# Two layers of a hybrid diffusion block: layer 1's modulation summed on VectorE during layer 0's FFN, and a token-major Fourier branch on half the spectrum

## The chip, the core and the metric

The kernel runs on one core of a Trainium2 chip. The metric is the device time of one execution in microseconds (us). Engines are named as in the profile: PE is TensorE's matrix multiply and PEld its weight load, DVE is VectorE, ACT is ScalarE, POOL is GpSimd, and SP is the sync engine, whose queue issues most DMAs.

## The reference, cut to what matters

Two layers work on 256 latent tokens and 256 context tokens of 1024 channels; in layer 1 the context feeds only keys and values. All is fp32.

```python
mod  = silu_c  @ w_mod + b_mod          # 6 blocks of 1024: sh1 sc1 gt1 sh2 sc2 gt2, for the latent tokens
modc = silu_cc @ w_mod[:, :n] + ...     # the same for the context: 6 blocks in layer 0, blocks 0 and 1 in layer 1
h    = modulate(x, g_norm1, sh1, sc1)   # rms_norm(x, g) * (1 + sc1) + sh1
proj = h @ w_in                         # keys/values, queries, Fourier columns (512), three gates
o_four = real(fft2(proj[fourier].reshape(b, l, 4, 128), axes=(tokens, channels of a group), norm="ortho"))
x = x + gt1 * (sum over MLA, GQA and Fourier of sigmoid(gate) * (o @ w_branch)) @ w_o
x = x + gt2 * conv_ffn(modulate(x, g_norm2, sh2, sc2))   # up (2 x 2816), width-3 conv, silu gate, down
```

The real part of a group's two-dimensional transform is C_tok F C_ch - S_tok F S_ch, with cosine and sine matrices over 256 tokens and 128 channels.

## The kernel before, in words

Tokens lie in the free dimension and channels on partitions for most of the work: 512 columns (latent and context) in layer 0, 256 in layer 1. Every large product is done in three matmuls, `mm3` (lines 104 to 106): each operand is split into a rounded part on ACT and a rest on DVE (`split`, lines 118 to 126), so each weight chunk of 128x1024 passes through one DMA of 512 KB, an ACT cast and a DVE subtraction. `wchunk` holds three raw chunks and three split ones. PSUM has eight banks under five tags: "mm", "s" and "pt" with two each, "o" and "tk" with one each.

**Modulation.** For a block of 1024 columns of w_mod the contraction over 1024 channels is eight slices k. `mod_burst` (line 238) takes two slices at a time, a quarter q of the block: two raw tiles of 128x1024, and for each slice four fp32 matmuls whose stationary operand is 32 columns of `cpad` (the two conditioning vectors, then others that are ignored) and whose outputs go to four groups of 32 partitions (line 254). Quarters are added into `row` on DVE (line 261), and after the fourth the row is transposed back to partitions, and b_mod is added (lines 269 to 274). Layer 0's blocks 0 and 1 are done at the very start by `mod_unit`. The others are handed to the layer as lists: "g" is emitted between the heads of the first attention (GQA), "m" between those of the second (MLA), "n1" and "n2" right after the first and second norm, and "f" behind every second column group of the FFN's up-projection. Layer 0 carries layer 1's block 1 in "n2" and its own block 5 and layer 1's block 0 in "f"; layer 1 carries its own blocks 2, 3, 4 and 5.

**Fourier branch.** In each of two halves (two groups of 128 channels) the columns are projected channel-major (`L0fp`), split, multiplied by the channel cosines and sines into `Y` (token-major, 128 tokens at a time), split, and then four products over tokens are summed for each 256 tokens into `Z`, which is split into the operand of the branch projection. The tables come through `load_dft` (line 1060): the channel table and four of 128x256 over tokens. Behind the branch in program order stand, in layer 0, the first attention with the Fourier gates `gF` ("mm" banks) and projections `bF` as fillers between heads; in layer 1, the latent projections ("mm" banks) and then the same.

**FFN.** In layer 0 the 22 column groups of the hidden width are done as 12, then their down-projection, then 10, then theirs; each down-projection runs over four chunks `mc` of 256 output channels. In the second one's last chunk the next layer's first norm starts between its two halves.

**Order.** A planner simulates the timeline and lays out each engine's instructions from it: on each engine the instruction that is ready and stands first in priority goes next, where priority is program order and `tc.high_priority(n)` lifts a part by n places. The order is fixed when the kernel is built; at run time every engine works through its list in order. Tiles with one tag share buffers in program order, so a new tile waits until the older one's readers are done.

Of the kernel before, what the change touches and what calls it, by code (L numbers as in the profile page):

```python
# [8 lines left out]
F32 = mybir.dt.float32  # L9
F32R = mybir.dt.float32r  # L10
# [20 lines left out]
RAWBUFS = 3  # L31
WBUFS = 3
RSQRT_MAGIC = 0x5F3759DF
MOD_AHEAD = 400


@with_exitstack
def hybrid_kernel(ctx: ExitStack, tc: tile.TileContext, a: dict, out: bass.AP):
# [196 lines left out]
    def mod_burst(l, blk, q, tags=None, bank="tk"):  # L235


        name = f"mod{l}"
        ps = pm(f"{name}_ps{blk}{q}", bank)
        raws = []  # L240
        for i in range(2):
            if tags:
                raw = S.tile([P, WMAX], F32, tag=tags[i], name=f"{name}_w{blk}{q}{i}")
            else:
                raw = wpool.tile([P, WMAX], F32, tag="mraw", name=f"{name}_w{blk}{q}{i}", bufs=2)
            k = 2 * q + i
            with after("qg0", l == 0 and blk == 2 and q == 0):
                nc.sync.dma_start(out=raw, in_=a["w_mod"][l, k * P:(k + 1) * P, blk * 1024:(blk + 1) * 1024])
            raws.append(raw)
        with tc.high_priority(MOD_AHEAD):  # L250
            for i in (1, 0):
                k = 2 * q + i
                for g in range(4):
                    nc.tensor.matmul(ps[32 * g:32 * g + 32, :256], cpad[:, 2 * k:2 * k + 32], raws[i][:, g * 256:(g + 1) * 256],  # L254
                                     start=i == 1, stop=i == 0, tile_position=(0, 32 * g))
        if q == 0:
            row = mod_rows[l, blk] = S.tile([P, 256], F32, tag="row", name=f"{name}_row{blk}", bufs=2)
            nc.scalar.copy(row, ps[:, :256])
# [148 lines left out]
    def layer(l, p, modT, last, xT, mods, prep, wkvg=None, norm=None):  # L407
# [146 lines left out]
        of_ = []  # L554
        with after("qg0"):
            dft = load_dft(l)
        for c in range(2):
            w = wchunk(w_in, 0, KD, FOUR_START + c * 256, 256, f"{n_}fo{c}")
            if last:
                ft = S.tile([P, 2, 2, TQ], F32R, tag=f"D{2 * c}", name=f"{n_}f{c}")  # L560
                fs = [ft[:, i] for i in range(2)]
            else:
                fs = [pair(f"D{2 * c + i}", f"{n_}f{c}{i}") for i in range(2)]
            fm_group(w, [0, P], KD, hs, TQ,
                     lambda i, ps: split(ps, fs[i][:, 0, :TQ], fs[i][:, 1, :TQ], later=True), f"{n_}fp{c}", "mm" if c == 0 else "o" if last else ("o", "tk"),
                     whole=lambda ps: split(ps.rearrange("p (i t) -> p i t", i=2), ft[:, :, 0, :], ft[:, :, 1, :]))
            Y = []
            for tt in range(NTQ):
                ps = pm(f"{n_}Y{c}{tt}", "s")
                ts = slice(tt * P, (tt + 1) * P)  # L570
                for i in range(2):
                    mm3(ps[:, i * 256:(i + 1) * 256], fs[i][:, 0, ts], fs[i][:, 1, ts],
                        dft[0][:, 0, :], dft[0][:, 1, :], True, True)
                y = pair(f"X{tt}", f"{n_}Y{c}{tt}")
                split(ps, y[:, 0, :], y[:, 1, :])
                Y.append(y)
            if last:
                zp = pm(f"{n_}Z{c}", "pt")
                zps = [zp[:, :TQ], zp[:, TQ:]]
            for i in range(2):  # L580
                ps = zps[i] if last else pm(f"{n_}Z{c}{i}", "pt")
                for s in range(NS):
                    n = 0
                    for t2 in range(2):
                        for cs in range(2):
                            y = Y[s * 2 + t2]
                            wsl = slice(i * 256 + cs * P, i * 256 + (cs + 1) * P)
                            q = 1 + t2 * 2 + cs
                            mm3(ps[:, s * 256:(s + 1) * 256], y[:, 0, wsl], y[:, 1, wsl],
                                dft[q][:, 0, :], dft[q][:, 1, :], n == 0, n == 3)  # L590
                            n += 1
                if not last:
                    o = pair(f"B{2 * c + i}", f"{n_}fo{c}{i}")
                    split(ps, o[:, 0, :], o[:, 1, :])
                    of_.append(o)
            if last:
                op = S.tile([P, 2, 2, TQ], F32R, tag=f"B{c}", name=f"{n_}fo{c}")
                split(zp.rearrange("p (i t) -> p i t", i=2), op[:, :, 0, :], op[:, :, 1, :])
                of_ += [op[:, 0], op[:, 1]]
# [341 lines left out]
        run_after(mods["n2"], before)  # L941
        nxt = []
        turn = None
        slots = ["B0", "B1", "B2", "B3", "D0", "D1", "D2", "D3", "D4", "Y0", "Y1", "E0", "E1"]
        per = 2 // NS
        for j0, jn in ((0, 12), (12, 10)) if not last else ((0, 22),):
            acts = []
            at_ = None
            for jj in range(jn):
# [42 lines left out]
                o = at_[:, jj % per]  # L992
                split(g[:, :TQ], o[:, 0, :], o[:, 1, :], 0.5)
                acts.append(o)
            for mc in range(4):
                ws = [wchunk(a["w_down"][l], j0 + k0, min(8, jn - k0), mc * 256, 256, f"{n_}dn{j0}{k0}{mc}")
                      for k0 in range(0, jn, 8)]

                def w(k, c, m):
                    return ws[k // 8](k % 8, c, m)  # L1000
                if last:
                    fm_group(w, [0, P], jn, acts, TQ, lambda i, ps: residual(mc * 2 + i, ps, 40),
                             f"{n_}dp{j0}{mc}", ("mm", "s")[mc % 2])
                    store(xn, mc)
                elif mc == 3 and j0:
                    fm_halves(w, [0, P], jn, acts, lambda i, s_, ps: residual_half(mc * 2 + i, s_, ps, 40), f"{n_}dp{j0}{mc}",
                              lambda: nxt.append(next_norm(xn)))
                else:
                    fm_group(w, [0, P], jn, acts, TQ, lambda i, ps: residual(mc * 2 + i, ps, 40),
                             f"{n_}dp{j0}{mc}", ("mm", "s")[mc % 2])  # L1010
# [48 lines left out]
    def load_dft(l):  # L1059

        d4 = S.tile([P, 2, 2, 256], F32R, tag="D4", name=f"dft{l}d")
        ts = [d4[:, 0], d4[:, 1]] + [S.tile([P, 2, 256], F32R, tag="pr", name=f"dft{l}{i}", bufs=3) for i in range(3)]
        for i, t in enumerate(ts):
            if i == 0:
                src = a["dft_d"]
            else:
                t2, cs = divmod(i - 1, 2)
                src = a["dft_s"][t2 * P:(t2 + 1) * P, cs * 256:(cs + 1) * 256]
            raw = S.tile([P, 256], F32, tag="ot", name=f"dft{l}r{i}", bufs=2)
            nc.sync.dma_start(out=raw, in_=src)  # L1070
# [22 lines left out]
    def next_norm(xn):  # L1093
# [3 lines left out]

    xT, nxt = layer(0, prm[0], modT[0], False, xT, {
        "n1": [], "g": bursts(0, 2) + bursts(0, 3), "m": bursts(0, 4),
        "n2": bursts(1, 1, (0, 1), ["Y0", "Y1", "Y2", "Y3"], "pt") + bursts(1, 1, (2, 3), None, "pt"),  # L1100
        "f": bursts(0, 5) + bursts(1, 0)}, [prep], w3)
    layer_params2(1, prm[1])
    layer(1, prm[1], modT[1], True, xT, {
        "n1": bursts(1, 2, (0, 1), ["Y1", "Y2", "Y3", "E1"], "pt"), "g": bursts(1, 2, (2, 3)) + bursts(1, 3), "m": bursts(1, 4),
        "n2": bursts(1, 5, range(4), free[8:], "pt"), "f": []}, [], None, nxt[0])

def _tables():
# [13 lines left out]
    def dft(n):  # L1123
# [38 lines left out]
```

## Time and profile before

| | us |
|---|---|
| median of 3 runs | 1423.36 (1422.74 to 1425.29) |
| profiled execution | 1422.24 |
| its span | 1420.4 |
| PE busy | 1379.5 |
| DVE busy | 892.4 |
| ACT busy | 662.2 |
| POOL busy | 332.9 |

The span runs from the first to the last instruction of the profiled execution. Busy times of different engines overlap. A matmul's recorded duration includes its way through the pipeline, so the distance between the starts of neighbours is the pace at which they are done, and the recorded duration is not.

### The profile page before, as it was taken

Reading aid. Unit: us, or ns where it says so; the run is one execution under the profiler, and the core shown is the slowest. Engines: PE = TensorE matmul, PEld = TensorE weight load, DVE = VectorE, ACT = ScalarE, POOL = GpSimd, SP = SyncE. Lnnn points to the kernel's source line nnn. Section 1 sums busy time; section 2 is a strip of 40 time slices with the busy share of each in tenths; the row PEclk is TensorE's granted clock in tenths of the full one; section 3 lists DMA queues with packets and bytes.
Section 4 is the critical chain, followed back from the end, with each engine's and each line's share of the span. In section 5 each row is a group of like instructions: output and inputs, shape, how many; then the busy total and the mean of one; then the engine's idle time right before and its main releaser. Section 6 shows DMA issues by size and latency. Waiting matters only on the chain.

```text
span 1420.4 us, 23006 instructions
## 1 busy us (share of the span) xinstructions
PE 1379.5 (97%) x8801; PEld 1195.3 (84%) x8801; DVE 892.4 (63%) x1644; ACT 662.2 (47%) x1164; POOL 332.9 (23%) x399
## 2 busy tenths in 40 slices
PE   6999999999999999999999999999998998999998
PEld 4988888878888788878678888899977998899998
DVE  5575655666645666655326663677687766788853
ACT  4434545435554344444114442445564663566642
POOL 3211323364323311101000111121245332112200
PEclk9999999999999999999999999999999999999999
DMA  9733442143321745343343232363744555466663
GB/s 318 247 89 105 148 146 73 54 120 106 90 74 38 262 149 197 101 148 104 104 134 91 87 99 91 111 177 95 229 134 140 155 176 188 129 180 186 184 191 121
DMA packets 163064, 197.97 MB, mean 139 GB/s; under 512 B 7144, under 2 KB 149530, under 8 KB 162954
## 3 DMA queue, kind: packets, MB, share of 16 engines
q1 hardware_dynamic: 161952, 195.85, 44.5%
q0 software_dynamic: 864, 0.61, 0.4%
q8 instruction: 69, 1.13, 0.3%
q14 instruction: 41, 0.34, 0.1%
q10 hardware_dynamic: 138, 0.04, 0.0%
HBM read 192.28 MB, written 3.15 MB: 138 GB/s over the span
## 4 chain that ended last, share of the span: by engine, by line
PE 89%; DVE 5%; DMA 2%; POOL 1%; issue 1%; ACT 1%; SPq 1%; DVEq 0%; ACTq 0%; POOLq 0%
PE L0upp L104 6%; PE L0upp L105 6%; PE L0upp L106 6%; PE mod_ps L254 3%; PE L1upp L104 3%; PE L1upp L105 3%; PE L1upp L106 3%; PE L0dp L106 3%; PE L0dp L104 3%; PE L0dp L105 3%; PE L0gp L106 3%; PE L0gp L104 3%; PE L0gp L105 3%; PE L1dp L106 1%; PE L1dp L104 1%; PE L1dp L105 1%
## 5 line engine op out<-in xcount | busy, mean ns | idle before, releaser
L104 PE MATMUL L0upp<-L0n_h,L0up_h 128*128 128x512 f32 (+1 forms) x384 | 141.7, 373 | 1.1 <-ACT L0n_h L332 1.1
L105 PE MATMUL L0upp<-L0n_h,L0up_h 128*128 128x512 f32 (+1 forms) x384 | 141.9, 373 | 0.0
L106 PE MATMUL L0upp<-L0n_h,L0up_l 128*128 128x512 f32 (+1 forms) x384 | 140.0, 373 | 0.0
L984 POOL TENSOR_TENSOR L0sg<-L0sg,L0u 128x512 f32<-128x512 f32 x22 | 31.4, 1426 | 288.6 <-DVE L0u L961 274.9
L104 PE MATMUL L1upp<-L1n_h,L1up_h 128*128 128x256 f32 x352 | 96.5, 286 | 1.1 <-ACT L1n_h L332 1.1
L106 PE MATMUL L1upp<-L1n_h,L1up_l 128*128 128x256 f32 x352 | 97.0, 285 | 0.0
L105 PE MATMUL L1upp<-L1n_h,L1up_h 128*128 128x256 f32 x352 | 96.4, 285 | 0.0
L124 DVE TENSOR_TENSOR L0up_l<-L0up_w,L0up_h 128x1024 fp32r<-128x1024 f32 x44 | 58.8, 1337 | 53.7 <-ACT L0up_h L118 50.6
L104 PEld LDWEIGHTS L0upp<-L0n_h,L0up_h 128*128 128x128 f32 x384 | 71.8, 188 | 15.4 <-issue 1.6
L106 PEld LDWEIGHTS L0upp<-L0n_h,L0up_l 128*128 128x128 f32 x384 | 72.1, 188 | 13.6 <-issue 0.8
L105 PEld LDWEIGHTS L0upp<-L0n_h,L0up_h 128*128 128x128 f32 x384 | 72.0, 188 | 13.5 <-issue 0.8
L118 ACT CAST L0up_h<-L0up_w 128x1024 fp32r<-128x1024 f32 x44 | 46.3, 1053 | 72.2 <-PE L0upp L105 49.7
L104 PE MATMUL L0gp<-L0n_h,L0g_h 128*128 128x512 f32 x192 | 76.3, 397 | 0.0
L105 PE MATMUL L0gp<-L0n_h,L0g_h 128*128 128x512 f32 x192 | 75.5, 393 | 0.0
L106 PE MATMUL L0gp<-L0n_h,L0g_l 128*128 128x512 f32 x192 | 75.2, 396 | 0.1
L106 PE MATMUL L0dp<-L0act,L0dn_l 128*128 128x512 f32 (+1 forms) x196 | 72.7, 371 | 0.0
L104 PE MATMUL L0dp<-L0act,L0dn_h 128*128 128x512 f32 (+1 forms) x196 | 72.6, 370 | 0.0
L105 PE MATMUL L0dp<-L0act,L0dn_h 128*128 128x512 f32 (+1 forms) x196 | 72.5, 370 | 0.0
L104 PEld LDWEIGHTS L1upp<-L1n_h,L1up_h 128*128 128x128 f32 x352 | 66.9, 194 | 1.5 <-ACT L1n_h L332 1.5
L106 PEld LDWEIGHTS L1upp<-L1n_h,L1up_l 128*128 128x128 f32 x352 | 67.3, 194 | 0.0
L105 PEld LDWEIGHTS L1upp<-L1n_h,L1up_h 128*128 128x128 f32 x352 | 66.8, 194 | 0.0
L124 DVE TENSOR_TENSOR L1up_l<-L1up_w,L1up_h 128x1024 fp32r<-128x1024 f32 x44 | 54.2, 1231 | 18.6 <-ACT L1up_h L118 17.2
(1534 smaller groups left out, 4322.9 us busy)
## 6 DMA issues: line engine op xcount, KB each, us to landing
mod_w<-in_w_mod_dram SPq DMA_DIRECT2D x96, 512.0 KB, 5.0
L0up_w<-in_w_up_dram SPq DMA_DIRECT2D x44, 512.0 KB, 3.6
L1up_w<-in_w_up_dram SPq DMA_DIRECT2D x44, 512.0 KB, 4.3
L0g_w<-in_w_in_dram SPq DMA_DIRECT2D x24, 512.0 KB, 3.7
L1g_w<-in_w_in_dram SPq DMA_DIRECT2D x24, 512.0 KB, 4.0
L0dn_w<-in_w_down_dram SPq DMA_DIRECT2D x20, 512.0 KB, 3.5
L1dn_w<-in_w_down_dram SPq DMA_DIRECT2D x16, 512.0 KB, 3.5
L0wo_w<-in_w_o_dram SPq DMA_DIRECT2D x8, 512.0 KB, 7.0
```

Source lines behind the costliest of these rows:

```text
L104: nc.tensor.matmul(ps, lh, rh, start=start, stop=False)
L105: nc.tensor.matmul(ps, lh, rl, start=False, stop=False)
L106: last_mm[0] = nc.tensor.matmul(ps, ll, rh, start=False, stop=stop).ins
L118: nc.scalar.copy(hi, src)
L124: nc.vector.tensor_sub(lo, src, f(hi))
L254: nc.tensor.matmul(ps[32 * g:32 * g + 32, :256], cpad[:, 2 * k:2 * k + 32], raws[i][:, g * 256:(g + 1) * 256], start=i == 1, stop=i == 0, ...
L984: nc.gpsimd.tensor_mul(g[:, :TQ], g[:, :TQ], us[1][:, :TQ])
```

## The change

Of layer 1's six modulation blocks, 0 to 4 are no longer bursts. For each slice k of 128 channels, DVE multiplies the raw 128x1024 weights by that slice's conditioning value, one per partition, and adds this to an accumulator; after eight slices the array sums the accumulator over its partitions with a column of ones (`opad`, shifted by one column per vector). Blocks 1 and 0 do it for two vectors, blocks 2, 3 and 4 for one, since layer 1 uses them for the latent tokens only. The 40 steps are emitted in layer 0's FFN: one behind each odd column group, and up to four ahead of each down-projection chunk. Layer 0's block 5 moves to its second norm; layer 1 keeps two quarters of its block 5 after each norm. `MOD_AHEAD` goes from 400 to 3000.

In the Fourier branch the projection is token-major, 512 columns at once. The token transform comes first, on a table of 129 cosine and 127 sine columns, into A (channels on partitions, half the spectrum's cosines and sines over tokens). The channel transform follows, as a product with the channel sines (`zs`) and one with the channel cosines (`zc`). Their sum gives tokens 1 to 127, their difference the mirrored tokens 255 to 129, and tokens 0 and 128 are copied.

```diff
-MOD_AHEAD = 400
+MOD_AHEAD = 3000
...
+    def mod_sums(l, blk, nv):
+        name = f"mod{l}"
+        accs = []
+        def step(k):
+            raw = wpool.tile([P, WMAX], F32, tag="mraw", name=f"{name}_w{blk}{k}", bufs=2)
+            nc.sync.dma_start(out=raw, in_=a["w_mod"][l, k * P:(k + 1) * P, blk * 1024:(blk + 1) * 1024])
+            if k == 0:
+                accs[:] = [S.tile([P, 1024], F32, tag=f"Y{2 + v}", name=f"{name}_acc{blk}{v}") for v in range(nv)]
+            for v, acc in enumerate(accs):
+                cv = cpad[:, 2 * k + v:2 * k + v + 1]
+                if k == 0:
+                    nc.vector.tensor_scalar(acc, raw, cv, None, ALU.mult)
+                else:
+                    nc.vector.scalar_tensor_tensor(acc, raw, cv, acc, op0=ALU.mult, op1=ALU.add)
+            if k < KD - 1:
+                return
+            ps = pm(f"{name}_ps{blk}", "tk")
+            with tc.high_priority(MOD_AHEAD):
+                for v, acc in enumerate(accs):
+                    for g in range(4):
+                        nc.tensor.matmul(ps[32 * g:32 * g + 32, :256], opad[:, 1 - v:33 - v], acc[:, g * 256:(g + 1) * 256],
+                                         start=v == 0, stop=v == nv - 1, tile_position=(0, 32 * g))
+            row = S.tile([P, 256], F32, tag="row", name=f"{name}_row{blk}", bufs=2)
+            nc.scalar.copy(row, ps[:, :256])
...
+        return [lambda k=k: step(k) for k in range(KD)]
...
-        for c in range(2):
...
+        w = wchunk(w_in, 0, KD, FOUR_START, 512, f"{n_}fo")
+        pss = [pm(f"{n_}fp{tt}", ("mm", "s")[tt // 2]) for tt in range(NTQ)]
+        for k0 in range(0, KD, 2):
+            for tt in range(NTQ):
+                ts = slice(tt * P, (tt + 1) * P)
+                for k in (k0, k0 + 1):
+                    wh, wl = w(k, 0, 512)
+                    mm3(pss[tt], hs[k][:, 0, ts], hs[k][:, 1, ts], wh, wl, k == 0, k == KD - 1)
+        ft = [pair(f"D{tt}", f"{n_}f{tt}") for tt in range(NTQ)]
+        for tt in range(NTQ):
+            split(pss[tt], ft[tt][:, 0, :], ft[tt][:, 1, :])
+        nb = 2 * NS
+        pss = [pm(f"{n_}A{b}", ("pt", "pt", "o", "tk")[b] if not last else "s") for b in range(nb)]
+        for s in range(NS):
+            for g in range(4):
+                b, hf = (g, s) if NS == 2 else divmod(g, 2)
+                gs = slice(g * P, (g + 1) * P)
+                for t2 in range(2):
+                    f_ = ft[s * 2 + t2]
+                    mm3(pss[b][:, hf * 256:(hf + 1) * 256], f_[:, 0, gs], f_[:, 1, gs],
+                        dft[1 + t2][:, 0, :], dft[1 + t2][:, 1, :], t2 == 0, t2 == 1)
+        As = [pair(f"X{b}", f"{n_}A{b}") for b in range(nb)]
+        for b in range(nb):
+            split(pss[b], As[b][:, 0, :], As[b][:, 1, :])
+        for b in range(nb):
+            ah, al = (As[b][:, i, :].rearrange("p (s k) -> p s k", s=2) for i in range(2))
+            zc = pm(f"{n_}Zc{b}", "mm" if not last else "pt")[:, :260].rearrange("p (s k) -> p s k", s=2)
+            zs = pm(f"{n_}Zs{b}", "s" if not last else ("o", "tk")[b])[:, :256].rearrange("p (s k) -> p s k", s=2)
+            mm3(zs, dft[0][:, 0, P:], dft[0][:, 1, P:], ah[:, :, P:], al[:, :, P:], True, True)
+            mm3(zc, dft[0][:, 0, :P], dft[0][:, 1, :P], ah[:, :, :130], al[:, :, :130], True, True)
+            zt = S.tile([P, 256], F32, tag="ot", name=f"{n_}zt{b}", bufs=2).rearrange("p (s k) -> p s k", s=2)
+            nc.scalar.copy(zt, zs)
+            z = S.tile([P, 512], F32, tag="pr", name=f"{n_}z{b}", bufs=3)
+            z3 = z.rearrange("p (s k) -> p s k", s=2)
+            nc.vector.tensor_add(z3[:, :, 1:P], zc[:, :, 1:P], zt[:, :, 1:])
+            nc.vector.tensor_sub(z3[:, :, 255:P:-1], zc[:, :, 1:P], zt[:, :, 1:])
+            nc.scalar.copy(z3[:, :, 0:P + 1:P], zc[:, :, 0:P + 1:P])
...
+                if j % 2:
+                    sums(1)
             for mc in range(4):
                 ws = [wchunk(a["w_down"][l], j0 + k0, min(8, jn - k0), mc * 256, 256, f"{n_}dn{j0}{k0}{mc}")
                       for k0 in range(0, jn, 8)]
+                sums(4)
...
-        "n2": bursts(1, 1, (0, 1), ["Y0", "Y1", "Y2", "Y3"], "pt") + bursts(1, 1, (2, 3), None, "pt"),
-        "f": bursts(0, 5) + bursts(1, 0)}, [prep], w3)
+        "n2": bursts(0, 5, (0, 1), ["Y0", "Y1", "Y2", "Y3"], "pt") + bursts(0, 5, (2, 3), None, "pt"), "f": [],
+        "v": [s for blk, nv in ((1, 2), (0, 2), (2, 1), (3, 1), (4, 1)) for s in mod_sums(1, blk, nv)]}, [prep], w3)
...
-        "n1": bursts(1, 2, (0, 1), ["Y1", "Y2", "Y3", "E1"], "pt"), "g": bursts(1, 2, (2, 3)) + bursts(1, 3), "m": bursts(1, 4),
-        "n2": bursts(1, 5, range(4), free[8:], "pt"), "f": []}, [], None, nxt[0])
+        "n1": bursts(1, 5, (0, 1), ["Y1", "Y2", "Y3", "E1"], "pt"), "g": [], "m": [],
+        "n2": bursts(1, 5, (2, 3), free[8:12], "pt"), "f": [], "v": []}, [], None, nxt[0])
```

## Rows read from the trace of the kernel before

**Rows 1.** The page: span, busy time by engine, chain of waits by engine.

```profile
span 1420.4 us, 23006 instructions
...
PE 1379.5 (97%) x8801; PEld 1195.3 (84%) x8801; DVE 892.4 (63%) x1644; ACT 662.2 (47%) x1164; POOL 332.9 (23%) x399
...
PE 89%; DVE 5%; DMA 2%; POOL 1%; issue 1%; ACT 1%; SPq 1%; DVEq 0%; ACTq 0%; POOLq 0%
```

**Rows 2.** Timeline of PE, layer 0's Fourier branch: start us, us, instruction.

```profile
107.80 0.39 PE L106 MATMUL L0gp<-L0n_h,L0g_l 128*128 128x512 f32 x1
...
108.71 0.39 PE L104 MATMUL L0gp<-L0n_h,L0g_h 128*128 128x512 f32 x1
108.94 0.28 PE L104 MATMUL L0Z<-dft0d,L0Y 128*128 128x256 f32 x1
...
110.85 0.28 PE L104 MATMUL L0Z<-dft,L0Y 128*128 128x256 f32 x1
```

**Rows 3.** Busy us (instructions) by stretch; then clock, DMA share, GB/s.

```profile
80.00:118.00 38.00, 38.00 (x241) 34.48 (x240) 24.30 (x40) 15.99 (x26) 4.97 (x10) 1.00 0.24 70
560.00:860.00 300.00, 300.00 (x1337) 237.91 (x1336) 158.15 (x194) 108.50 (x133) 27.80 (x20) 1.00 0.36 111
640.00:740.00 100.00, 100.00 (x422) 74.61 (x421) 38.92 (x50) 24.85 (x28) 5.75 (x4) 1.00 0.36 112
980.00:1046.00 66.00, 65.80 (x544) 58.57 (x544) 46.71 (x88) 40.02 (x82) 16.33 (x16) 1.00 0.59 186
1066.00:1092.00 26.00, 20.29 (x157) 18.06 (x156) 19.74 (x33) 10.20 (x17) 14.77 (x15) 0.95 0.55 171
1092.00:1172.00 80.00, 79.78 (x647) 74.69 (x646) 56.51 (x100) 49.72 (x96) 27.40 (x26) 0.99 0.49 151
```

**Rows 4.** Timeline of PE, one burst and the matmul behind it.

```profile
122.83 1.07 PE L254 MATMUL mod_ps<-mod_w,cpad 128*32 128x256 f32 x16
123.83 0.50 PE L104 MATMUL L0bp<-L0fo,L0b_h 128*128 128x512 f32 x1
```

**Rows 5.** The bursts alone (line 254) by stretch; 16 records are one burst.

```profile
980.00:1140.00 160.00, 10.71 (x160) 4.17 (x160) 0.99 0.53 161
```

**Rows 6.** Timeline, layer 1's second norm.

```profile
1213.88 1.96 PE L254 MATMUL mod_ps<-mod_w,cpad 128*32 128x256 f32 x32
...
1214.65 0.87 DVE L914 SCALAR_TENSOR_TENSOR L1xk<-L1o,modT,L1xk 128x256 f32<-128x256 f32 x2
...
1215.76 0.38 PE L316 MATMUL L1n_ss<-ones,L1n_sa 128*128 128x1 f32 x2
...
1220.45 0.70 PE L326 MATMUL L1n_rb<-L1n_dg,ones 128*128 128x256 f32 x2 [0.40 <-DVE L1n_dg L325]
```

**Rows 7.** Groups on DVE, 560 to 900 us: busy us, mean ns, idle before.

```profile
L124 DVE TENSOR_TENSOR L0up_l<-L0up_w,L0up_h 128x1024 fp32r<-128x1024 f32 x37 | 49.5, 1337 | 47.2 <-ACT L0up_h L118 46.9
...
L983 DVE SCALAR_TENSOR_TENSOR L0sg<-L0sg,L0u 128x512 f32<-128x512 f32 x19 | 13.1, 688 | 8.3 <-ACT L0sg L982 8.3
...
L261 DVE TENSOR_TENSOR mod_row<-mod_row,mod_ps 128x256 f32<-128x256 f32 x4 | 1.7, 414 | 5.5 <-PE mod_ps L254 5.5
```

**Rows 8.** Groups on DVE, 440 to 480 us.

```profile
L124 DVE TENSOR_TENSOR L0wo_l<-L0wo_w,L0wo_h 128x1024 fp32r<-128x1024 f32 x4 | 7.2, 1818 | 0.0
```

**Rows 9.** The token transform's result tile in layer 0: ns min/median/max.

```profile
L104 PE MATMUL L0Z<-dft,L0Y x24: 280/283/283, 97.5 to 116.1; 128*128 128x256 f32 x24
...
L104 PE MATMUL L0Z<-dft0d,L0Y x8: 277/283/283, 94.8 to 113.5; 128*128 128x256 f32 x8
...
L124 DVE TENSOR_TENSOR L0fo<-L0Z,L0fo x4: 690/691/691, 102.6 to 117.3; 128x512 fp32r<-128x512 f32 x4
```

**Rows 10.** Chain of waits, layer 1's first norm: start us, us, what.

```profile
920.07 0.24 PE L1kvg L105
...
926.07 0.13 PE L1kvg L104
```

**Rows 11.** What PE waited for: us in total, times, longest.

```profile
PE L1m0tq L872 <- POOL L1qtok L460: 4.6, 2, 2.5
```

More of the change, by code (lines that the diff above doesn't have):

```diff
@@ L275, in mod_burst @@
         return turn
+    def mod_sums(l, blk, nv):
[22 more added lines that the diff above has]
+            nc.scalar.copy(row, ps[:, :256])
+            tp = ps[:, 256:]
+            n = 96 + nv
+            for j in range(2):
+                nc.tensor.transpose(tp[:, j * P:j * P + n], row[:n, j * P:(j + 1) * P], ident[:n, :n])
+            for v in range(nv):
+                nc.vector.tensor_add(
+                    modT[l][:, v, blk * 8:(blk + 1) * 8].rearrange("p (g j) -> p j g", j=2),
+                    tp.rearrange("p (j g r) -> p j g r", j=2, g=4)[:, :, :, v],
+                    prm[l]["vec"][:, blk * 8:(blk + 1) * 8].rearrange("p (g j) -> p j g", j=2))
+        return [lambda k=k: step(k) for k in range(KD)]
     def scale_shift(l, sc0, sh0, g, nv):
@@ L556, in layer @@
             dft = load_dft(l)
-        for c in range(2):
-            w = wchunk(w_in, 0, KD, FOUR_START + c * 256, 256, f"{n_}fo{c}")
+        w = wchunk(w_in, 0, KD, FOUR_START, 512, f"{n_}fo")
[6 more added lines that the diff above has]
+                    mm3(pss[tt], hs[k][:, 0, ts], hs[k][:, 1, ts], wh, wl, k == 0, k == KD - 1)
@@ L559, in layer @@
             if last:
-                ft = S.tile([P, 2, 2, TQ], F32R, tag=f"D{2 * c}", name=f"{n_}f{c}")
-                fs = [ft[:, i] for i in range(2)]
-            else:
[L563 to L599, printed above, removed]
+                op = S.tile([P, 2, 2, TQ], F32R, tag=f"B{b}", name=f"{n_}fo{b}")
+                split(z3, op[:, :, 0, :], op[:, :, 1, :])
+                of_ += [op[:, 0], op[:, 1]]
+            else:
+                o = pair(f"B{b}", f"{n_}fo{b}")
+                split(z, o[:, 0, :], o[:, 1, :])
+                of_.append(o)
@@ L943, in layer, with sums @@
         turn = None
+        def sums(n):
+            for step in mods["v"][:n]:
+                step()
+            del mods["v"][:n]
         slots = ["B0", "B1", "B2", "B3", "D0", "D1", "D2", "D3", "D4", "Y0", "Y1", "E0", "E1"]
@@ L1034, in hybrid_kernel @@
     nc.vector.tensor_mul(cpk, csrc, cth)
+    opad = const.tile([P, 33], F32, name="opad")
+    nc.vector.memset(opad, 0.0)
+    nc.vector.memset(opad[:, 1:2], 1.0)
     xt0 = [S.tile([P, 2, 512], F32, tag=f"X{i}", name=f"x0{i}") for i in range(4)]
@@ L1061, in load_dft @@
         d4 = S.tile([P, 2, 2, 256], F32R, tag="D4", name=f"dft{l}d")
-        ts = [d4[:, 0], d4[:, 1]] + [S.tile([P, 2, 256], F32R, tag="pr", name=f"dft{l}{i}", bufs=3) for i in range(3)]
+        ts = [d4[:, 0], d4[:, 1], S.tile([P, 2, 256], F32R, tag="pr", name=f"dft{l}", bufs=3)]
         for i, t in enumerate(ts):
@@ L1066, in load_dft @@
             else:
-                t2, cs = divmod(i - 1, 2)
-                src = a["dft_s"][t2 * P:(t2 + 1) * P, cs * 256:(cs + 1) * 256]
+                src = a["dft_s"][(i - 1) * P:i * P, :]
             raw = S.tile([P, 256], F32, tag="ot", name=f"dft{l}r{i}", bufs=2)
@@ L1132, in _tables @@
         "dft_d": np.concatenate([cd, sd], axis=1).astype(np.float32),
-        "dft_s": np.concatenate([cs, -ss], axis=1).astype(np.float32),
+        "dft_s": np.concatenate([cs[:, :129], -ss[:, 1:128]], axis=1).astype(np.float32),
     }
```

## The prediction

> **What bounds the kernel now.** I read the page's busy shares first, then the chain of waits, then the stretches, then single instructions. The page shows TensorE (PE) busy 97% of the 1420.4 us, VectorE (DVE) 63%, and a chain that ended last of which 89% is PE [rows 1]. A PE that is busy need not be at its peak, so the paces come from the timeline: 128x512 matmuls start every 0.227 us (107.80 to 108.71 are four of them) and 128x256 ones every 0.12 us (108.94 to 110.85 are sixteen) [rows 2]. In layer 0's FFN and in most of layer 1's attention PE has no gap: 300.00 of 300, 65.80 of 66, 79.78 of 80 us; only 1066 to 1092 has a hole of 5.7 us [rows 3]. So this kernel's time is the sum of its matmul paces plus some 41 us (1420.4 - 1379.5) in which PE waits, and an edit is worth what it takes out of PE in a stretch without gaps.
>
> **The profiled execution.** It took 1422.24 us around a span of 1420.4; the median of the runs shown is 1423.36, 1.1 us more. I sum against 1422.2 and add 1.1 at the end.
>
> **Modulation: what goes.** Today a quarter of a 1024-column block is a "burst": 8 fp32 matmuls, recorded as 16, that take 1.00 us of PE (122.83 until the next matmul at 123.83) [rows 4]. Of layer 1's 24 bursts the change keeps block 5's four. Blocks 0 to 4, 20 bursts, become sums on DVE. Each block ends in four fp32 matmuls per conditioning vector: blocks 1 and 0 (two vectors) 8, as many as one burst, 1.0 us; blocks 2, 3, 4 (one vector) 4, 0.5 us if the pace holds; it can't be under that share, and a whole burst's 1.0 bounds it above. I take 2 x 1.0 + 3 x 0.5 = 3.5 us (up to 5.0): the same four column tiles in the same order. The transposes at a block's end stay as many, only earlier.
>
> In layer 0's FFN 12 bursts stand now: layer 1's block 1 beside the norm, layer 0's block 5 and layer 1's block 0 further on. Afterwards four remain (block 5, in block 1's old place). So -8 + 3.5 = **-4.5 us**, PE having no gap there [rows 3].
>
> In layer 1's attention 10 go, the 160 records at 980 to 1140 [rows 5]: six are handed to the first attention, four to the second. I take nine to lie where PE is full and one in or beside the stretch in which PE waits anyway. So **-9 us** (between 0, if VectorE and GpSimd set that stretch, and -10).
>
> At layer 1's second norm four bursts become two. They are fill: the last projection's residual on DVE starts at 1214.65 while two bursts run, the sums of squares start only at 1215.76, the other two bursts run while DVE works out the square root, and PE still waits 0.40 us before the broadcast at 1220.45 [rows 6]. I cost the removal at **0** (at best -0.8: two of DVE's 0.41 us row additions [rows 7] leave the chain). DMA: the same 512 KB loads, 24 more of them on the sync engine's queue in the FFN, 12 fewer in layer 1's attention and norm; with buffers two deep, and weights three deep in front of PE, I count none.
>
> **Modulation: what comes.** 40 steps, 16 with two DVE instructions and 24 with one: 56 of 128x1024 fp32. The trace has no such sum. The nearest in form is the 128x512 scalar_tensor_tensor in SBUF, 0.688 us; the nearest in width is the 128x1024 split, 1.34 us in the FFN [rows 7], 1.82 us at 440 to 480 where GpSimd is busy [rows 8]. I take 1.34: 75 us; bounds 56 x 0.688 = 39 and 56 x 1.82 = 102. In the FFN's stretch from 560 to 860 DVE is busy 158.1 of 300 us [rows 3], so 142 us stand idle there, plus the tail; 75 fits, 102 fits. The tightest place is the first down-projection, where 20 steps are issued, 10 of them double: 30 x 1.34 = 40 us on top of 38.9 in 100 [rows 3] (the stretch reaches a little past it). PE takes a weight chunk every 24 x 0.227 = 5.4 us and three chunks are held, so a sum in front of a split delays it inside its slack. The price on the path is **0**; if the cover goes, each sum that a needed split waits behind costs its 1.34 us.
>
> **Fourier branch, layer 0.** The projection becomes token-major: 96 matmuls of 512 columns before and after. Behind it, before: 48 (channel transform) + 96 (token transform) of 256 columns; the second group's rows stand three times each, 3 x 24 + 3 x 8 [rows 9]. After: 48 + 24 (12 of 256, 12 of 260). 72 fewer x 0.12 = -8.6 us. DVE and ACT keep about the same: 16 evacuations of 512 columns go to 12, and three half-width additions or copies plus a narrow one come for each of four groups; two table loads and their splits go.
>
> What is lost: slack. Now the gates of the Fourier branch fill PE between the transform's matmuls (0.227 us steps up to 108.71, the transform from 108.94) [rows 2], since they take the "mm" banks, which the transform does not use. Afterwards the cosine half sits in those two banks, so group 2 waits until group 0 is combined, and the gates wait until groups 2 and 3 are. One group costs DVE 0.69 (split in) [rows 9] + 2 x 0.42 (the 128x256 addition of the bursts, 0.415 [rows 7]) + 0.69 (split out) = 2.2 us against PE's 6 x 0.12 = 0.72. Four groups: 8.9 us of DVE from the end of the first, 2.1 us of PE in the rest of the first transform and 2.9 in the second. Splits out may be late, which leaves 6.1 us of DVE against 5.0 of PE, and the copies on ScalarE run ahead of it. So 1.1 us at least, 3.9 at most without filler; a burst (1 us), transposes and other heads fill some. I take a stall of 2.5: **-6.1 us**. Bounds: no stall, -8.6; a stall of 6 with weight splits between, -2.6.
>
> **Fourier branch, layer 1.** Half the tokens: 72 become 36, -36 x 0.12 = -4.3; the projection's 96 of 256 become 48 of 512, 96 x 0.12 - 48 x 0.227 = -0.6. Its second half uses other banks than the latent projections that follow, so I charge 1.5 us of latency: **-3.4 us** (0 to -4.9).
>
> **Sum.** -4.5 - 9 - 0 - 6.1 - 3.4 = -23.0. 1422.2 - 23.0 = 1399.2, plus 1.1: **1400 us**.
>
> **Rivals.**
> *A, everything is filled.* The planner lays bursts and other heads into the Fourier gaps and the norm gains its 0.8: -4.5 - 10 - 0.8 - 8.6 - 4.9 = -28.8, 1394.5. For it: PE shows no gap at all in today's branch (38.00 of 38) [rows 3]. Against: the shared banks.
>
> *B, the Fourier gaps grow until the clock falls.* Stalls of 6 and 4 us in place of 2.5 and 1.5, and after each a stretch at the lower clock. In layer 1's first norm PE waited 1.83 and 1.18 us, and its 288-column matmuls then came every 0.24 us (920.07) until, at 926.07, they were back at 0.13 [rows 10]; from 919.46 to 925.8 that halves the pace and costs some 3 us. So 6 + 2 x 3 = +12: 1412. For: the branch has become three stages in a row on one set of banks. Against: each wait there is 1 to 2 us and the banks come free one by one. The Trainium skill ("TensorE: Matmul & The Clock Gate", section "Why this matters for your kernels") warns against TensorE idling between bursts of matmuls, because it is then throttled to half rate; by that rule B's second part follows from its first. The trace agrees (0.24 against 0.13 us).
>
> *C, layer 1's attention is set by VectorE and GpSimd.* PE waits 4.6 us for GpSimd's query rotation [rows 11] and 5.7 us in all at 1066 to 1092 [rows 3]. If that chain starts no earlier, the 9 us come back as waiting: 1409. Against: DVE is busy 46.7 of 66 us ahead of it, so it can start earlier with PE.
>
> *D, the sums stand in front of the weight splits (slower).* Place: DVE's queue in layer 0's down-projections; DVE works in order, so a sum whose modulation load is late, or four in a row, holds back a split, the residual that frees a PSUM bank, and with them PE. Each such sum costs 1.34 us; above 23/1.34 = 17 of the 56 the kernel is slower than before. With 30 of them: 1400 + 40 = 1440. For: four steps are issued together there, and their final matmuls rank far ahead on PE's order, where a late sum blocks all behind it. Against: DVE's 61% idle in that stretch and the three chunks held.
>
> *E, not there.* If the planner moved the sums out of layer 0's FFN, DVE's load there would not rise; it has no reason to, as they need only loads and two tiles that are free by then.
>
> **Chances.** The sum as above 40%, A 24%, B 14%, C 10%, B and C together 4% (1400 + 12 + 9 = 1421, which is no change), D 8%. A measurement of this kernel can tell about 0.2%, 2.8 us, from no change. Faster: 0.88; same: 0.04; slower: 0.08. The range takes in A with a little below it for the bounds of the stalls, and B: 1390 to 1413; B with C and D, 12%, are left outside, and some of the tails.
>
> **What would show it.** Right: bursts of 1.0 us gone from 980 to 1140; 56 DVE instructions of about 1.3 us in layer 0's FFN, PE still without gaps there and the FFN 4 to 5 us shorter; the sums' last matmuls 0.5 or 1.0 us per block; 72 and 36 fewer transform matmuls; PE holes of 1 to 4 us behind the channel transform; layer 1's second norm as long as now. Wrong: PE waiting for a weight split or a sum in the FFN (D); a granted clock under 1.00 near 110 us (B); a hole at layer 1's key and query tokens that has grown by what the attention saved (C); sums much over 1.82 us each.

## The result, and the profile after

Timed side by side, the changed kernel takes 1407.78 us (median of four, 1404.45 to 1410.51), the kernel before 1423.98 (1422.74 to 1425.29): ratio 0.9885, 95% interval 0.9862 to 0.9909, so about 16 us (13 to 20) are gone where 23 were forecast. The profiled execution, the fastest of the four, took 1404.45 us around a span of 1402.7, 17.7 under the span of before.

The page, the lines that answer to [rows 1]:

```profile
span 1402.7 us, 22232 instructions
...
PE 1348.4 (96%) x8381; PEld 1177.3 (84%) x8381; DVE 945.7 (67%) x1686; ACT 660.3 (47%) x1166; POOL 337.5 (24%) x399
...
PE 86%; DVE 7%; DMA 2%; issue 2%; POOL 1%; ACT 1%; SPq 0%; DVEq 0%; ACTq 0%; POOLq 0%
```

PE is busy for 31.1 us less, but the time falls by only 17.7: its idle time rose from 41 to 54 us, and DVE's share of the chain from 5% to 7%. Where the two part shows in the stages. Each boundary is the start of the first matmul of a named tile (L0fp, L0upp, L1kvg, L1fp, L1ukv, L1m0s, L1o, L1upp); us in the profiled executions:

| from ... to | before | after | difference | forecast |
|---|---|---|---|---|
| layer 0 Fourier, attention, output (70.9 / 71.0 on) | 449.4 | 444.8 | -4.6 | -6.1 |
| layer 0 FFN, next norm begun | 387.8 | 389.1 | **+1.3** | **-4.5** |
| layer 1 projections before the Fourier branch | 33.3 | 32.9 | -0.4 | 0 |
| layer 1 Fourier and six bursts | 94.2 | 86.4 | -7.8 | |
| layer 1 keys and queries | 55.9 | 55.2 | -0.7 | |
| layer 1 heads | 90.8 | 87.3 | -3.5 | |
| the last three together | | | -12.0 | -12.4 |
| layer 1 output projection and second norm | 40.0 | 37.8 | -2.2 | 0 |

Busy us by stretch, as in [rows 3] (PE, PEld, DVE, ACT, POOL, then clock, DMA share, GB/s; the layer 1 stretches now end at the boundaries of the table):

```profile
80.00:118.00 38.00, 35.39 (x184) 30.19 (x183) 25.71 (x47) 15.88 (x31) 5.30 (x10) 0.96 0.19 56
...
515.80:560.00 44.20, 35.80 (x245) 31.60 (x245) 41.20 (x65) 17.48 (x30) 5.44 (x4) 0.85 0.60 183
560.00:860.00 300.00, 299.71 (x1351) 245.17 (x1350) 211.37 (x257) 112.70 (x144) 34.51 (x22) 1.00 0.48 150
640.00:740.00 100.00, 99.71 (x446) 81.61 (x445) 61.67 (x71) 29.23 (x34) 6.80 (x4) 1.00 0.57 176
...
980.00:1024.20 44.20, 44.20 (x357) 43.20 (x356) 32.59 (x59) 28.13 (x50) 9.80 (x9) 1.00 0.44 127
1024.20:1079.40 55.20, 46.02 (x289) 40.77 (x288) 45.54 (x94) 31.24 (x65) 29.04 (x34) 0.93 0.35 103
1079.40:1166.70 87.30, 87.30 (x684) 84.28 (x684) 60.50 (x99) 55.30 (x104) 32.14 (x29) 0.98 0.42 129
```

PE is full through the FFN from 560 on, the first down-projection included (99.71 of 100, DVE 61.67). The hole is earlier, in layer 0's second norm and first up-projection: 8.4 of 44.2 us idle, and a granted clock of 0.85 over the stretch. The same work before had neither:

```profile
520.30:560.00 39.70, 39.68 (x309) 34.48 (x310) 30.01 (x64) 20.01 (x35) 6.53 (x6) 1.00 0.58 201
```

What PE waited for there, in the kernel after (us in total, times, longest):

```profile
PE mod_ps L300 <- DVE mod_acc L293: 2.8, 2, 2.3
PE L0upp L105 <- POOL L0n_h L373: 2.4, 1, 2.4
PE L0upp L105 <- DVE L0n_h L375: 1.6, 1, 1.6
```

DVE's timeline says why. The sums (lines 291, 293) begin between the norm's own small steps (lines 369, 375), before DVE has evacuated any up-projection (line 1006, first at 548.05), although the program issues them behind that evacuation:

```profile
524.12 1.42 DVE L291 TENSOR_SCALAR mod_acc<-mod_w,cpad 128x1024 f32<-128x1024 f32 x2 [1.04 <-DMA mod_w<-in_w_mod_dram]
525.45 0.48 DVE L369 SCALAR_TENSOR_TENSOR L0n_t<-L0x,L0A,L0n_rb 128x256 f32<-128x256 f32 x1
...
530.35 2.48 DVE L293 SCALAR_TENSOR_TENSOR mod_acc<-mod_w,cpad,mod_acc 128x1024 f32<-128x1024 f32 x2
532.74 0.47 DVE L369 SCALAR_TENSOR_TENSOR L0n_t<-L0x,L0A,L0n_rb 128x256 f32<-128x256 f32 x1
...
538.71 5.35 DVE L293 SCALAR_TENSOR_TENSOR mod_acc<-mod_w,cpad,mod_acc 128x1024 f32<-128x1024 f32 x4
545.65 2.48 DVE L293 SCALAR_TENSOR_TENSOR mod_acc<-mod_w,cpad,mod_acc 128x1024 f32<-128x1024 f32 x2 [1.59 <-DMA mod_w<-in_w_mod_dram]
548.05 0.74 DVE L1006 SCALAR_TENSOR_TENSOR L0u<-L0upp,cw,L0u 128x510 f32<-128x510 f32 x1
```

A norm step of 0.48 us is followed by 2.5 us of sums, so the normalised tiles reach PE late. Up to 560, 20.6 us of the sums are done there. The waits on line 300 are of another kind: PE stands 2.3 us before the first block's last matmuls, because the sums that they read end late, and DVE itself stood 1.59 us before one pair of these (545.65) until its load had landed.

The groups on DVE that answer to [rows 7]: the sums cost 75.7 us, as forecast (75), the 49 fused ones 1456 ns and the seven plain ones 745:

```profile
L293 DVE SCALAR_TENSOR_TENSOR mod_acc<-mod_w,cpad,mod_acc 128x1024 f32<-128x1024 f32 x49 | 70.6, 1456 | 9.5 <-DMA mod_w<-in_w_mod_dram 9.5
L291 DVE TENSOR_SCALAR mod_acc<-mod_w,cpad 128x1024 f32<-128x1024 f32 x7 | 5.1, 745 | 1.0 <-DMA mod_w<-in_w_mod_dram 1.0
```

In layer 0's Fourier branch PE does the cosine half of group 2 without a wait (101.75: group 0 gave its bank up with the copy of 101.53 below). It stands before that of group 3, which needs the bank that group 1 holds, and afterwards the gates, 0.227 us apart in [rows 2], come every 0.43 us until 109:

```profile
101.75 0.39 PE L104 MATMUL L0Zc<-L0A,dft0d 128*128 128x260 f32 x1
...
104.99 0.39 PE L104 MATMUL L0Zc<-L0A,dft0d 128*128 128x260 f32 x1 [2.61 <-ACT L0z L633]
...
106.44 0.63 PE L104 MATMUL L0gp<-L0n_h,L0g_h 128*128 128x512 f32 x1
106.86 0.63 PE L105 MATMUL L0gp<-L0n_h,L0g_h 128*128 128x512 f32 x1
...
109.58 0.39 PE L106 MATMUL L0gp<-L0n_h,L0g_l 128*128 128x512 f32 x1
109.81 0.39 PE L104 MATMUL L0gp<-L0n_h,L0g_h 128*128 128x512 f32 x1
```

The copy that ends the wait, of group 1's tokens 0 and 128, is short (0.17 us) but stands on ACT behind four casts for the attention keys; group 1's additions on DVE were done at 102.10:

```profile
101.53 0.17 ACT L633 COPY L0z<-L0Zc 128x4 f32<-128x4 f32 x1 [0.98 <-DVE L0z L632]
...
102.40 0.58 ACT L836 CAST L0KG<-L0gk 64x512 fp32r<-64x512 f32 x1
...
104.17 0.58 ACT L837 CAST L0KG<-L0gk 64x512 fp32r<-64x512 f32 x1
104.78 0.17 ACT L633 COPY L0z<-L0Zc 128x4 f32<-128x4 f32 x1
```

In layer 1's attention no instruction of line 254 is left ([rows 5]). In its second norm, [rows 6], two bursts remain, and the wait before the broadcast has grown from 0.40 to 2.19 us, by about what the other two covered:

```profile
1195.93 1.96 PE L254 MATMUL mod_ps<-mod_w,cpad 128*32 128x256 f32 x32
...
1202.20 1.19 PE L364 MATMUL L1n_rb<-L1n_dg,ones 128*128 128x256 f32 x2 [2.19 <-DVE L1n_dg L363]
```

### The profile page after: what moved, and what is told of

It is laid out like the page before. It is cut to its first block, busy times and chain, and to the rows that moved or that the text cites. A ratio compares the mean times of both kernels' runs of the same rounds, so it can differ in the third digit from the quotient of the medians.

```text
span 1402.7 us, 22232 instructions
## 1 busy us (share of the span) xinstructions
PE 1348.4 (96%) x8381; PEld 1177.3 (84%) x8381; DVE 945.7 (67%) x1686; ACT 660.3 (47%) x1166; POOL 337.5 (24%) x399
## 4 chain that ended last, share of the span: by engine, by line
PE 86%; DVE 7%; DMA 2%; issue 2%; POOL 1%; ACT 1%; SPq 0%; DVEq 0%; ACTq 0%; POOLq 0%
PE L0upp L106 5%; PE L0upp L104 5%; PE L0upp L105 5%; PE L1upp L104 3%; PE L1upp L105 3%; PE L1upp L106 3%; PE L0gp L106 3%; PE L0dp L104 3%; PE L0gp L105 3%; PE L0dp L105 3%; PE L0dp L106 3%; PE L0gp L104 3%; PE L1dp L106 1%; PE L1dp L105 1%; PE L1dp L104 1%
## 5 line engine op out<-in xcount | busy, mean ns | idle before, releaser
L105 PE MATMUL L0upp<-L0n_h,L0up_h 128*128 128x512 f32 (+1 forms) x384 | 144.8, 380 | 4.0 <-POOL L0n_h L373 2.4
L104 PE MATMUL L0upp<-L0n_h,L0up_h 128*128 128x512 f32 (+1 forms) x384 | 144.2, 379 | 2.6 <-ACT L0n_h L370 1.1
L1031 POOL TENSOR_TENSOR L0sg<-L0sg,L0u 128x512 f32<-128x512 f32 x22 | 34.5, 1571 | 275.6 <-DVE L0u L1008 255.6
L105 PEld LDWEIGHTS L0upp<-L0n_h,L0up_h 128*128 128x128 f32 x384 | 74.0, 193 | 17.8 <-POOL L0n_h L373 2.6
L104 PEld LDWEIGHTS L0upp<-L0n_h,L0up_h 128*128 128x128 f32 x384 | 73.6, 193 | 16.5 <-ACT L0n_h L370 1.5
L124 DVE TENSOR_TENSOR L0up_l<-L0up_w,L0up_h 128x1024 fp32r<-128x1024 f32 x44 | 55.9, 1269 | 32.6 <-ACT L0up_h L118 32.3
L293 DVE SCALAR_TENSOR_TENSOR mod_acc<-mod_w,cpad,mod_acc 128x1024 f32<-128x1024 f32 x49 | 70.6, 1456 | 9.5 <-DMA mod_w<-in_w_mod_dram 9.5
L106 PE MATMUL L0gp<-L0n_h,L0g_l 128*128 128x512 f32 x192 | 75.7, 400 | 0.0
L104 PEld LDWEIGHTS L1upp<-L1n_h,L1up_h 128*128 128x128 f32 x352 | 67.1, 195 | 1.8 <-ACT L1n_h L370 1.8
L124 DVE TENSOR_TENSOR L1up_l<-L1up_w,L1up_h 128x1024 fp32r<-128x1024 f32 x44 | 54.2, 1232 | 18.9 <-ACT L1up_h L118 17.5
```

What stands on the lines that cost most here:

```text
L104: nc.tensor.matmul(ps, lh, rh, start=start, stop=False)
L105: nc.tensor.matmul(ps, lh, rl, start=False, stop=False)
L106: last_mm[0] = nc.tensor.matmul(ps, ll, rh, start=False, stop=stop).ins
L124: nc.vector.tensor_sub(lo, src, f(hi))
L293: nc.vector.scalar_tensor_tensor(acc, raw, cv, acc, op0=ALU.mult, op1=ALU.add)
L1031: nc.gpsimd.tensor_mul(g[:, :TQ], g[:, :TQ], us[1][:, :TQ])
```

## The experiments

The theory from the two traces has three parts. (1) *Pulled sums*: the planner puts the sums' DVE instructions into the latency of layer 0's second norm, and that costs about 12 us. (2) *Broken bursts*: in the kernel before two of the FFN's bursts were not 1.0 us but many times that, so the removal alone, or the longer lead MOD_AHEAD, is worth about 10 us that the forecast did not see. (3) *Shared banks*: the cosine halves of groups 2 and 3 wait for groups 0 and 1. The rivals: the sums' loads delay the weights; the lead has no effect; ACT's queue, whatever the bank, sets the Fourier stretch. The expectations below speak of a stall at group 2; by the rows above it is group 3's.

Stages are read from one profiled execution of each kernel. Where the kernels do the same work a stage can still differ: the stretch ahead of L0fp takes 70.8 to 74.2 us in the ten profiles, with either lead, and layer 1's output projection with its norm 34.8 to 40.0.

Part (2) is read from the kernel before, PE between 676 and 681 us:

```profile
676.58 0.39 PE L105 MATMUL L0dp<-L0act,L0dn_h 128*128 128x512 f32 x1
676.90 0.62 PE L254 MATMUL mod_ps<-mod_w,cpad 128*32 128x256 f32 x2
677.45 0.50 PE L106 MATMUL L0dp<-L0act,L0dn_l 128*128 128x512 f32 x1
...
679.09 0.62 PE L254 MATMUL mod_ps<-mod_w,cpad 128*32 128x256 f32 x2
679.64 0.49 PE L106 MATMUL L0dp<-L0act,L0dn_l 128*128 128x512 f32 x1
680.06 0.62 PE L254 MATMUL mod_ps<-mod_w,cpad 128*32 128x256 f32 x2
```

A burst whole has its 16 records in a row and takes 1.00 us [rows 4]. This one stands in eight pieces of two records, each between two weight matmuls, and so does a second (pieces from 706.19 to 713.25). A piece with one weight matmul takes some 0.975 us (0.97 from 679.09 to 680.06, others 0.98); less the matmul's 0.227 that is 0.745 a piece, 6.0 a burst.

**ahead3000**: the kernel before with the longer lead alone.

```diff
-MOD_AHEAD = 400
+MOD_AHEAD = 3000
```

> The kernel before with MOD_AHEAD at 3000 and nothing else. Theory (broken bursts): two of the bursts in layer 0's FFN before stand in eight pieces, one between every two weight matmuls, and each piece takes 0.975 us where a weight matmul alone takes 0.227, so such a burst costs PE 6.0 us and not 1.0; the larger head start keeps it whole. So about 10 us less than before: 1414. Rival (head start without effect, all of the gain is the sums' and the Fourier branch's): 1424, no change.

Measured: 1412.82 us against 1421.04, ratio 0.9932 [0.9906, 0.9958], 9.7 us. The FFN's stage goes from 387.8 to 378.2. The FFN's bursts on PE, 160 records both times, before and then in this kernel (busy us, mean ns):

```profile
L254 PE MATMUL mod_ps<-mod_w,cpad 128*32 128x256 f32 x160 | 18.5, 386 | 0.0
```

```profile
L254 PE MATMUL mod_ps<-mod_w,cpad 128*32 128x256 f32 x160 | 10.7, 385 | 0.0
```

10.7 is ten whole bursts. Shown: in the kernel before, one constant, which does no work of its own, is worth about 9.7 of the 16 us that the whole change gains. It does not follow that it carries as much in the change, which takes the two broken bursts away with either lead; ahead400 below measures it there.

**m_only** and **f_only**: the two halves of the change alone, m_only with the lead at 3000, f_only with 400.

```diff
 m_only:
-MOD_AHEAD = 400
+MOD_AHEAD = 3000
...
+    def mod_sums(l, blk, nv):
...
+                if j % 2:
+                    sums(1)
 f_only:
-        for c in range(2):
-            w = wchunk(w_in, 0, KD, FOUR_START + c * 256, 256, f"{n_}fo{c}")
+        w = wchunk(w_in, 0, KD, FOUR_START, 512, f"{n_}fo")
...
+            zc = pm(f"{n_}Zc{b}", "mm" if not last else "pt")[:, :260].rearrange("p (s k) -> p s k", s=2)
```

> The modulation part of the change alone, with the Fourier branch of before. Theory: the Fourier part gave 4.5 us in layer 0 and about 2 in layer 1, so this one lies 6 to 7 us above the changed kernel, at 1414. Rival (the Fourier part gave its forecast 9.5): 1417. Rival (the Fourier part gave nothing behind the sums' delay): 1408.

> The Fourier part of the change alone, with the modulation of before. Theory: PE loses some 4.3 us to the shared banks and the clock in layer 0 and about 3 in layer 1, out of 13.5 that were taken from it, so 6 to 7 us less than before: 1417. Forecast on record for this part: -9.5, 1414.5. Rival (the gaps eat all of it): 1424.

Measured: m_only 1412.52 us, ratio 0.9919 [0.9892, 0.9947], -11.5 us (its runs spread from 1403.23 to 1413.65, and its median is only 8.5 under before); f_only 1415.31, 0.9957 [0.994, 0.9974], -6.1. Within these intervals the halves add up to the whole, 17.6 for 16.4. m_only's gain can't be told from that of its constant alone: its FFN takes 388.2 us, while in layer 1 the ten bursts are worth 10.8 (5.9 + 0.8 + 4.1 in the three stages). f_only gains 3.4 in layer 0's branch and 2.2 in layer 1's; its other stages moved by up to 5 us either way, and why was not followed.

**hold1**: the change, the sums' DVE instructions queued behind the convolution of the second column group.

```diff
             for step in mods["v"][:n]:
-                step()
+                with after("up1"):
+                    step()
...
+                    if jc == NJ + 1:
+                        marks["up1"] = marks["cv"]
```

> The changed kernel with the sums' VectorE instructions queued behind the second column group's convolution, so that none stands inside layer 0's second norm. Theory (pulled sums): the planner drew the first sums into the norm's gaps, they held back the normalized tiles, and PE lost 8.4 us of waiting and about 3 at the lower clock between 516 and 560 us; without them 9 to 11 us less than the changed kernel: 1397 to 1399. Rival (the modulation loads in the sync engine's queue hold back the up-projection's weights): the loads stay where they are, 1406 to 1408.

Measured: 1394.97 us, ratio 0.9819 [0.9789, 0.985], 25.7 us under before; the interval lies clear of the change's. The FFN's stage is 376.0 in place of 389.1. The stretch that had the hole, and the one that took the sums:

```profile
517.20:560.00 42.80, 42.57 (x288) 38.30 (x288) 36.73 (x61) 22.89 (x36) 6.77 (x6) 1.00 0.40 132
560.00:860.00 300.00, 299.48 (x1355) 243.26 (x1356) 219.61 (x263) 109.83 (x141) 35.09 (x22) 1.00 0.51 162
```

Same 56 instructions, and PE is full in both. Later they do fit, as forecast. The other kernels bear this out: where the sums are pulled (the change, m_only, fz, ahead400) the FFN takes 386.5 to 390.1 us, where they are held or thin 376.0 to 376.8.

**thin**: tells DVE's time from the loads.

```diff
-                    nc.vector.scalar_tensor_tensor(acc, raw, cv, acc, op0=ALU.mult, op1=ALU.add)
+                    nc.vector.scalar_tensor_tensor(acc[:, :8], raw[:, :8], cv, acc[:, :8], op0=ALU.mult, op1=ALU.add)
```

> The change, but 49 of the sums' 56 DVE instructions (the fused multiply-adds) work on 8 of 1024 columns; all 40 loads stay. What it leaves out: most of the modulation sums of layer 1's blocks 0 to 4. Theory (DVE time of the sums pulled into layer 0's second norm and first up-projection holds PE back): DVE loses 49 x 1.46 = 71 us, the hole of 8.4 us of PE between layer 0's first up-projection at 516 and 560 and the low clock in it go, and layer 0's FFN comes to about 377 us in place of 389: 1394 to 1398 us, ratio 0.979 to 0.983. Rival (the 40 loads of 512 KB queue ahead of the weights on the sync engine's queue and these are late): the hole stays, 1404 to 1409, ratio 0.987 to 0.990.

Measured: 1396.72 us against 1421.33, ratio 0.9825 [0.9811, 0.9839]; the FFN's stage 376.8.

```profile
518.60:560.00 41.40, 40.23 (x287) 35.71 (x288) 33.44 (x76) 20.62 (x35) 7.31 (x6) 1.00 0.70 226
```

The loads come faster than in the change (226 GB/s against 183) and the hole is 1.2 us. That the loads make the hole by holding back the weights is refuted; DVE's time makes it.

**fz**: the cosine halves of groups 2 and 3 in banks that the token transform has left.

```diff
-            zc = pm(f"{n_}Zc{b}", "mm" if not last else "pt")[:, :260].rearrange("p (s k) -> p s k", s=2)
+            zc = pm(f"{n_}Zc{b}", "mm" if not last and b < 2 else "pt")[:, :260].rearrange("p (s k) -> p s k", s=2)
```

> The change, but in layer 0 the cosine halves of groups 2 and 3 go to the pt banks, which the channel transform has left by then, in place of the two mm banks that groups 0 and 1 hold. Theory (the shared banks make the stall of 2.6 us at group 2 and the half pace behind it): the wait at the cosine half of group 2 and the granted clock of 0.91 in 100 to 120 us go, and layer 0's first up-projection starts 3 to 4 us earlier: ratio 0.985 to 0.987, some 1404 us where the change has 1407.8. Rival (the chain of copies on ACT behind the gates' casts and of additions on DVE sets this stretch whatever the bank): the stall moves to the first gate, which then still waits for group 2's and 3's chain: a gain of 0 to 1 us, ratio 0.988 to 0.989.

Measured: 1401.07 us, ratio 0.9856 [0.9841, 0.9871]. Stretch 100 to 120, the change and then fz:

```profile
100.00:120.00 20.00, 17.39 (x91) 13.69 (x89) 11.04 (x21) 10.15 (x23) 1.59 (x2) 0.91 0.09 23
```

```profile
100.00:120.00 20.00, 20.00 (x113) 16.24 (x112) 13.68 (x25) 12.24 (x28) 2.11 (x3) 1.00 0.23 60
```

No wait is left, the clock is full, and the stage to the first up-projection takes 439.4 us in place of 444.8. ACT's copy comes as late as before, behind the same casts; PE runs the first gate meanwhile:

```profile
102.26 0.47 PE L104 MATMUL L0gp<-L0n_h,L0g_h 128*128 128x512 f32 x1
...
105.12 0.17 ACT L633 COPY L0z<-L0Zc 128x4 f32<-128x4 f32 x1
```

So ACT's queue alone does not set this stretch; the wait takes the shared bank and the late copy together. Whether moving the copy ahead of the casts would do as well was not run. By the ratios fz is 4.1 us under the change; the two intervals overlap, so the stage carries the verdict, and best1 below repeats it.

**ahead400**: the change with the old lead.

```diff
-MOD_AHEAD = 3000
+MOD_AHEAD = 400
```

> The change, with the priority lead of the modulation matmuls back at 400. Theory (a lead of 400 lets the planner break a row of column-tiled fp32 matmuls into pieces that stand one by one between weight matmuls, at some 0.75 us a piece in place of 0.125): of the five blocks' last matmuls, 32 in all, those of at least two blocks are broken: 8 to 16 pieces at 0.6 us more each, 5 to 10 us over the change: ratio 0.992 to 0.995. Rival (the sums' matmuls become ready only when their sum is done, at a moment with nothing else ahead of them, and stay whole; only the old bursts broke): within 1.5 us of the change, ratio 0.988 to 0.990.

Measured: 1410.82 us, ratio 0.9923 [0.9911, 0.9935]. Eight pairs of the last matmuls' records stand alone again, one by one between weight matmuls; four of them begin here:

```profile
792.43 0.62 PE L300 MATMUL mod_ps<-mod_acc,opad 128*32 128x256 f32 x2
792.99 0.49 PE L106 MATMUL L0upp<-L0n_h,L0up_l 128*128 128x512 f32 x1
793.41 0.62 PE L300 MATMUL mod_ps<-mod_acc,opad 128*32 128x256 f32 x2
```

The pieces are there, at the pace of before (0.98 us with the matmul): 8 x (0.745 - 0.125) = 5 us. The size is less clear: by the ratios it is 5.4 us over the change, but the intervals lie only 0.0002 apart, and the profiled FFN is only 1.0 us longer (390.1). Of the 8.0 us between the two spans 3.2 lie ahead of L0fp, which the lead doesn't explain.

**best1**: hold1 and fz together.

> The sums held behind the second column group's convolution (as in the run that held them) and the cosine halves of groups 2 and 3 in the pt banks, together. If both causes are real and independent: 12 us from holding and 3 to 4 from the banks off the change's 1407.8, some 1391 to 1393, ratio 0.977 to 0.979. Rival (the time freed in the Fourier branch is given back before layer 0's FFN, where DVE sets the norms): as the kernel with held sums alone, ratio 0.981 to 0.983.

Measured: 1391.78 us (1388.97 to 1395.5) against 1421.33, ratio 0.9793 [0.9775, 0.981], 29.4 us: the lowest median of all, though its interval overlaps hold1's. Its stage from L0fp to L0upp takes 439.5 (hold1 445.7), its FFN 376.5: both repairs hold side by side.

## Why the prediction was right, and which steps were not

The forecast of 1400 us was 8 too low (5.3 between the profiled executions), inside its range and with the right sign, but two larger errors of opposite sign stand behind it, both in layer 0's FFN: a gain of 9.9 us that it did not see and a loss of 13.1 that it priced at nothing. That they nearly cancel is luck.

*What bounds the kernel* held: where PE was full, taken-out work came off one for one. In the two full stages of layer 1's attention m_only has 9.8 us less PE work and takes 10.0 less; at keys and queries, where PE waits, 2.9 less work gave 0.8.

*Modulation, what goes (layer 0's FFN)*: -4.5 was forecast; it was +1.3, the sum of two errors.
- "each burst takes 1.0 us" was read from one instance, and two of the ten in this stretch took 6.0. With the sums held (hold1) the stage gives -11.8: eight bursts at 1.0, -8.0; the two broken ones, -9.9 more; the blocks' last matmuls +4.5 (hold1's busy time, 3.5 forecast); six more transpose records there +1.0; one late weight split +0.8. Together -11.6.
- "The price on the path is 0" failed by 13.1 us (389.1 - 376.0). The room was there (142 us of DVE idle from 560 to 860, and hold1 uses it), but the step asked only where the program issues the sums, not where the planner queues them. They need only loads and two free tiles, so they were put into every gap in front of that place. Of the 13.1, 7.9 are PE's waits (8.4 + 0.3 less hold1's 0.8), and a clock of 0.85 over 35.8 us of work makes some 5.

*Modulation, what comes*: 75 us for 56 sums, measured 75.7.

*Layer 1's attention and Fourier branch*: -9 - 3.4, measured -12.0, a sum that fits better than its terms. Without the Fourier part (m_only) the three stages gave -10.8, not -9, which leaves -1.2 for the Fourier branch; in f_only its own stage gave -2.2. PE waits 2.7 us in that stage now, 0.2 before, where 1.5 of latency was charged.

*Second norm*: priced 0 because the bursts were fill; the wait of 2.19 us took their place and the gap from the output projection to the up-projection went from 8.6 to 8.8. The output projection itself took 2.4 us less, unforeseen: in its second 10 us the clock was 0.85 before and is 1.00 after; since this stage differs by more among the other profiles, no cause is shown.

*Layer 0's Fourier branch*: that a cosine half waits for a bank which an earlier group holds, and the gates behind it, was right. It is group 3 that waits, for group 1, and not group 2 for group 0; and what ends the wait is a copy on ACT, where the sum counted DVE's instructions and said that "the copies on ScalarE run ahead of it". That copy ran 2.7 us after DVE was done (102.10 to 104.78). The term "stall of 2.5" was mis-sized, 5.4 by fz: the wait was 2.6, and the lower clock behind it, which the forecast had left to rival B, cost about 0.2 on each of some eight gates; the rest was not followed. The gain without it is -10.0 in this stage, not -8.6; the other 1.4 was not followed either.

*Rivals.* B came in part, in the named place with the named sign (clock 0.91 from 100 to 120) at less than half its price. The clock fell behind both holes, to 0.91 and 0.85 on the mean of their stretches (in them it stands at 0.50, the lower of its two levels, 1.2 of 2.4 GHz, from 106 to 109 and from 554 to 558), and is full again where fz and hold1 remove them. By the Trainium skill's rule quoted there ("TensorE: Matmul & The Clock Gate", section "Why this matters for your kernels") TensorE is throttled after it idles; the traces agree. C came weakly: at keys and queries PE's work shrank by 2.5 us and the time by 0.7. The wait of [rows 11] became

```profile
PE L1m2tk L909 <- DVE L1m1k L126: 3.6, 1, 3.6
PE L1m0tq L914 <- POOL L1qtok L498: 2.4, 2, 2.0
```

D was right in its mechanism (a sum in front of what PE needs, a last matmul that blocks PE, 2.8 us) and wrong in its place: the down-projections, where it looked for 1.34 us a sum, have no wait; the norm ahead of the FFN has.

## What to carry to other kernels

Under a planner new low-priority work runs where its inputs are ready, not where it is written: look upstream for the first stretch in which that engine has short gaps but sets the pace, and queue the work behind an instruction past it. Price what you remove from all its instances, by the form and the busy time of the group, not from one good one. And give a new stage banks that an earlier one has left before you let its groups take turns on two.

## What the runs showed of the hardware

Two fp32 matmul records on a 32-column tile cost 0.125 us in a row of sixteen and 0.745 us alone between full 128-column matmuls. The difference, some 0.62 us, is what going there and back cost. The Trainium skill ("TensorEngine Tiling (Array Packing)", section "Key Properties") says that changing the tiling mode drains TensorE; the traces agree with that, though no run here isolates the drain. On DVE, 1024 fp32 columns took 745 ns in a tensor_scalar and 1279 ns (median; 2311 at most) in a scalar_tensor_tensor, so a sum's first term costs little more than half of each later one.
